# Forming all low weight parts on VectorE in a split-precision trunk layer, with the heads of one indexer visit turned

## The chip, the cores and the metric

The kernel runs on one core of a Trainium2 chip. The metric is device time in microseconds (us) of one execution. The engines named below are TensorE (PE, its weight loads PEld), VectorE (DVE), ScalarE (ACT), GpSimd (POOL) and SyncE (SP), which here only issues loads.

## The reference

One layer of a causal decoder trunk on x of 256 rows by 1024 columns, everything in 32-bit floats. Cut to what matters:

```python
proj = x @ w_in[i]                       # one projection, columns of all mixers
o_a = dsa_mixer(...)                     # 8 indexer heads -> top-k keys, 6 heads, one k and v
o_b = dilated_mixer(...)                 # 3 groups x 4 heads over shared k, v
o_c = moba_mixer(...)                    # 6 heads, causal (256 rows are a single block)
gates = sigmoid(x @ w_gate[i])           # 1024 x 3072
merged = gates_a*(o_a@w_br_a) + gates_b*(o_b@w_br_b) + gates_c*(o_c@w_br_c)
x = layer_norm(ALPHA*x + merged @ w_out)
h = square(relu(x @ w_up)) @ w_down      # 1024 -> 4096 -> 1024
ple = sigmoid(x @ w_ple_gate) * (p @ w_ple)
x = layer_norm(ALPHA*x + h + ple)
```

The indexer computes `index = sum over heads of iw * relu(iq . ik)` and keeps the best 64 keys of each row; attention of the first mixer is masked to these.

## The kernel before

**Products in two parts.** Each 32-bit product is made of three faster ones. A matrix w is split into a rounded high part (`whi`) and the rest (`wlo` = w − `whi`); x likewise into `xh` and `xl`. TensorE adds up hi·hi, hi·lo and lo·hi in PSUM (function `prod`, matmuls of L189, 128x256 each).

**Weight units.** Weights come from HBM as units of at most 512 KB (128x1024), each loaded by SyncE into one of five `raw` buffers. `Weights._split` (L95 to L126) then copies the unit on ScalarE to `whi` (L112, L110 later) and subtracts to get `wlo` (L119 where the part lies in one piece, L123 where it lies in pieces of 128 columns, class `Apart`, whose `runs` joins equally spaced pieces into one instruction). The subtraction is divided by columns: 0 to c on VectorE and c to n on GpSimd, with

```python
c = n if by == "v" else by * n // 1024
```

The first 58 units get `by` from `add` (L215): 640 (the constant `DV`, L41), and 615 for c units; all later ones get "v", VectorE alone. A unit is split four units before its use (`AHEAD`), and a part pool of five buffers holds them.

**The order of units.** The table `TASKS` (L44) lists them: 18 units of the q/k projections (numbers), 24 gate units (g, 1024 columns), 8 units of two branch matrices (c, 640 columns), 4 units each of value projections (va, 656 columns; vb, 768), then 4 of branch a (768) and 4 of the output matrix. A g or q/k unit is laid out as five pieces 160 columns apart and three pieces 128 apart; 640 is where that spacing changes. `fill` puts g and c units between the heads of attention.

**Around attention.** `feat` makes the queries and keys of a pair of heads; `logits` (L336) makes the scores of one or two pairs with 128x128 and 128x256 matmuls (L347). Its first matmul is free, and all that follow are held in program order among TensorE's instructions that are so pinned. The indexer loop (L508 to L518) calls it twice, each time for two pairs, and adds each head's part to `idx` (L515 on VectorE, L518 on GpSimd). Of each later head: bias and maximum on VectorE (L416), exponentials on ScalarE (L419), the reciprocal of the sum (L406, VectorE), scaling (L408, ScalarE), transposes on TensorE (L388), the split of the transposed probabilities (L389 ScalarE, L390 VectorE), the products with v (L392, L393), their sum from PSUM (L396 ScalarE, L397 and L398 VectorE), and for a pair its split (L401 ScalarE, L402 VectorE), which is the operand `op` of the c and a units. A g unit ends in a sigmoid step (L311 ScalarE) and, with branch products, a gated sum (L326, L327 on VectorE). After that come the output product, layer norm, the up and down matrices, and the last norm.

**What sets the order.** Each engine's instruction order is made by a scheduler that plays the program on modelled durations; priorities (`high_priority`), pins (`keep_in_program_order`) and `issue_after` bind it. A changed duration or engine in one step therefore also moves other instructions.

Of the kernel before, what the change touches and what calls it, by code (L numbers as in the profile page):

```python
# [37 lines left out]

AHEAD = 4
FIRST = 4  # L40
DV = 640  # L41


TASKS = ("4 va 5 g 6 7 g 8 g g 9 g 10 11 g 12 g g vb g 13 14 g g 15 16 g g 17 18 g g "  # L44
# [99 lines left out]
def hybrid_layer(ctx: ExitStack, tc: tile.TileContext, x0, xn, pT, wqk, wva, wvb, wg, wbc, wba,  # L144
# [33 lines left out]
    t = banks.tile([128, 512], F32, name="b4", tag="b4")  # L178
# [52 lines left out]
    for t in TASKS:  # L231
        if t == "va":
            u_va = [add(wva[i], 656) for i in range(4)]
        elif t == "vb":
            u_vb = [add(wvb[i], 768, at=(56, 56)) for i in range(4)]
        elif t in "gcao":
            u, w, n = {"g": (u_g, wg, 1024), "c": (u_bc, wbc, 640), "a": (u_ba, wba, 768),
                       "o": (u_out, wout, 1024)}[t]
            u.append([add(w[len(u)], n, at=(40, LOW[t]) if t in LOW else (0, 0),
                          by=615 if t == "c" else DV)])  # L240
        else:
            u_q.append([add(wqk[int(t) - FIRST], 1024, at=(40, LOW["g"]))])

# [89 lines left out]
            next(side, None)  # L333
        return ps

    def logits(k, *qs):  # L336


        ss = [next(ps_s if n < 3 else ps_t)[:, 0:384] for n in range(2 * len(qs))]
        with tc.high_priority(offset=500):  # L340
            for b in range(2):
                c = slice(b * 128, (b + 1) * 128)
                for n, q in enumerate(qs):
                    for i, (x, y) in enumerate(((1, 0), (0, 0), (0, 1))):
                        for h in (1, 0):
                            d = slice(64 * h, 64 * h + 64)
                            m = pe.matmul(ss[2 * n + h][:, QC[b]], lhsT=q[d, x, c],  # L347
                                          rhs=k[d, y, 0:128 * (b + 1)], start=i == 0, stop=i == 2)
                            if b or n or i or not h:
                                tc.keep_in_program_order(m)  # L350
        return ss

# [115 lines left out]
    with ExitStack() as begin:  # L468
# [25 lines left out]
        iq = [q_pair(ps, 0.125) for ps in first]  # L494
# [3 lines left out]
    kI, kA = k_pair(ps[0:64], ps[0:64]), k_pair(ps[64:128], ps[64:128])  # L498
# [7 lines left out]

    values(u_va, 328, 0, 5, True)
    for j in range(4):  # L508
        s = s[2:] if j % 2 else logits(kI, iq[j], iq[j + 1])
        r = wk2.tile([128, 768], F32, name="ri", tag="eb")  # L510
        r = r.rearrange("p (h k) -> p h k", h=2)
        for h in range(2):
            act.activation(r[:, h], s[h], AF.Relu)
            n = 2 * j + h
# [21 lines left out]
    for j in range(2):  # L536
        ps = feat(5 + 4 * j)
        k = k_pair(ps)
        fill("g")
        qs = []  # L540
# [16 lines left out]
    for j in range(3):  # L557
        ps = feat(13 + 2 * j)
        k = k_pair(ps)
# [566 lines left out]
```

## Time and profile before

| | |
|---|---|
| runs, us | 428.67, 430.38, 428.92 (median 428.92) |
| profiled execution, us | 428.66 (span 426.9) |
| granted TensorE clock | 0.998 |
| busy, share of span | PE 98%, PEld 89%, DVE 82%, ACT 65%, POOL 28% |
| HBM | 84.30 MB moved, 197 GB/s mean |

The span runs from the first to the last instruction; 1.76 us of the execution lie outside it. POOL's busy time stands mostly in one group, the 50 subtractions of L123 with 68.4 us. In the rows shown below the two leading numbers are start and duration in us, "x3" counts joined instructions, and what stands in brackets is the idle time just before and the instruction that ended it.

### The profile page before, as it was taken

How to read it: one execution, taken by the hardware profiler on the slowest of the kernel's cores; microseconds unless marked ns; L12 is line 12 of the kernel's file. 1: busy time of each engine (PE TensorE's matmuls, PEld its weight loads, DVE VectorE, ACT ScalarE, POOL GpSimd, SP SyncE). 2: the span in 40 equal slices, each digit the busy share in tenths (PEclk: the TensorE clock that was granted, in tenths of full speed). 3: DMA queues.
4: the chain of work that ended last, by engine and by line, in shares of the span. 5: the costliest groups of instructions: out<-in, count | busy, mean ns of one | idle time of the engine just before them, and what ended most of it. 6: DMA issues, size and time to landing. Idle time of an engine off the chain costs nothing.

```text
span 426.9 us, 7810 instructions
## 1 busy us (share of the span) xinstructions
PE 417.1 (98%) x2804; PEld 378.1 (89%) x2804; DVE 351.1 (82%) x645; ACT 279.6 (65%) x531; POOL 118.9 (28%) x127
## 2 busy tenths in 40 slices
PE   8999999999999999999999999999999999999993
PEld 8989999999999999999887888888888888788883
DVE  5968758898676689879967889989998798999755
ACT  6777385585888777858414668887888666567310
POOL 1668474173544556500010002242220000000001
PEclk9999999999999999999999999999999999999999
DMA  8895966567463327587851776785665376646402
GB/s 294 301 327 161 286 222 189 164 201 269 130 181 126 131 63 259 145 267 276 292 206 49 236 257 197 210 291 191 187 207 152 117 266 216 190 147 230 164 2 99
DMA packets 28157, 84.30 MB, mean 197 GB/s; under 512 B 2977, under 2 KB 6985, under 8 KB 27733
## 3 DMA queue, kind: packets, MB, share of 16 engines
q1 hardware_dynamic: 26880, 79.54, 57.0%
q10 hardware_dynamic: 1140, 4.19, 2.8%
q8 instruction: 22, 0.36, 0.4%
q14 instruction: 19, 0.15, 0.1%
q0 software_dynamic: 96, 0.06, 0.0%
HBM read 81.88 MB, written 1.90 MB: 196 GB/s over the span
## 4 chain that ended last, share of the span: by engine, by line
PE 78%; DVE 5%; DMA 4%; issue 2%; ACT 2%; SPq 0%; POOLq 0%; DVEq 0%; POOL 0%; ACTq 0%
PE mm L189 34%; PE b L189 19%; PE mm L891 14%; PE mm L893 7%; DMA xr<-in_wdn_dram 4%; PE b L347 2%; DVE wlo L119 2%; PE b L388 1%; PE b L392 1%; ACT whi L112 1%; DVE Y L853 1%; ACT ri L517 1%; PE b L393 0%; DVE wlo L123 0%; DVE st L701 0%
## 5 line engine op out<-in xcount | busy, mean ns | idle before, releaser
L112 ACT CAST whi<-raw 128x1024 fp32r<-128x1024 f32 (+3 forms) x92 | 89.9, 988 | 38.2 <-PE b L189 14.7
L123 DVE TENSOR_TENSOR wlo<-raw,whi 128x256 fp32r<-128x256 f32 (+3 forms) x118 | 96.4, 840 | 16.6 <-ACT whi L112 13.9
L189 PE MATMUL mm<-xh,whi 128*128 128x256 f32 x336 | 90.2, 280 | 0.0
L189 PE MATMUL mm<-xl,whi 128*128 128x256 f32 x336 | 88.1, 278 | 0.0
L123 POOL TENSOR_TENSOR wlo<-raw,whi 128x384 fp32r<-128x384 f32 (+1 forms) x50 | 68.4, 1377 | 70.2 <-ACT whi L112 65.5
L189 PE MATMUL mm<-xh,wlo 128*128 128x256 f32 x336 | 80.6, 281 | 0.2 <-DVE k L299 0.2
L189 PEld LDWEIGHTS mm<-xh,whi 128*128 128x128 f32 x336 | 63.1, 188 | 0.8
L891 PE MATMUL mm<-x,whi 128*128 128x512 f32 x256 | 63.4, 389 | 0.0
L189 PEld LDWEIGHTS mm<-xl,whi 128*128 128x128 f32 x336 | 63.1, 188 | 0.1
L189 PEld LDWEIGHTS mm<-xh,wlo 128*128 128x128 f32 x336 | 57.8, 188 | 0.8 <-DVE k L299 0.4
L189 PE MATMUL b<-whi,store 128*128 128x512 f32 x168 | 54.1, 389 | 0.0
L891 PEld LDWEIGHTS mm<-x,whi 128*128 128x128 f32 x256 | 45.7, 188 | 7.5
L119 DVE TENSOR_TENSOR wlo<-raw,whi 128x1024 fp32r<-128x1024 f32 (+2 forms) x38 | 43.2, 1159 | 3.7 <-ACT whi L112 3.6
L708 POOL TENSOR_TENSOR rs<-rs,half 128x1 f32<-128x1 f32 x4 | 3.4, 843 | 147.5 <-DVE rs L707 147.5
L110 ACT CAST whi<-raw 128x256 fp32r<-128x256 f32 x64 | 36.9, 617 | 10.0 <-PE mm L891 5.4
L189 PEld LDWEIGHTS b<-whi,store 128*128 128x128 f32 x168 | 31.5, 188 | 6.4
L893 PEld LDWEIGHTS mm<-x,wlo 128*128 128x128 f32 x256 | 33.8, 188 | 2.5
L893 PE MATMUL mm<-x,wlo 128*128 128x256 f32 x256 | 34.2, 276 | 0.0
L189 PE MATMUL b<-wlo,store 128*128 128x512 f32 x84 | 32.8, 391 | 0.3 <-DVE wlo L119 0.3
L914 POOL TENSOR_TENSOR a<-a 128x128 f32<-128x128 f32 x7 | 5.3, 757 | 61.5 <-ACT a L877 55.6
L189 PE MATMUL mm<-op,whi 128*128 128x256 f32 x128 | 22.4, 280 | 0.0
L189 PE MATMUL b<-whi,x 128*128 128x512 f32 x64 | 20.5, 395 | 0.0
(223 smaller groups left out, 824.2 us busy)
## 6 DMA issues: line engine op xcount, KB each, us to landing
raw<-in_wup_dram SPq DMA_DIRECT2D x32, 512.0 KB
raw<-in_wg_dram SPq DMA_DIRECT2D x24, 512.0 KB
raw<-in_wqk_dram SPq DMA_DIRECT2D x18, 512.0 KB
raw<-in_wdn_dram SPq DMA_DIRECT2D x18, 512.0 KB
raw<-in_wout_dram SPq DMA_DIRECT2D x8, 512.0 KB
raw<-in_wpg_dram SPq DMA_DIRECT2D x8, 512.0 KB
T<-tabd SPq DMA_DIRECT2D x24, 128.0 KB
xr<-in_wdn_dram SPq DMA_DIRECT2D x6, 512.0 KB
```

The costliest lines, as they stand in the source:

```text
L110: i = nc.scalar.copy(blocks(hi, a, b), blocks(r, a, b))
L112: i = nc.scalar.copy(hi, r)
L119: i = e.tensor_tensor(lo[:, x], r[:, x], hi[:, x].bitcast(F32), op=ALU.subtract)
L123: i = e.tensor_tensor(blocks(lo, *x), blocks(r, *x), blocks(hi, *x).bitcast(F32), op=ALU.subtract)
L189: i = pe.matmul(ps, lhsT=a[x], rhs=b[y], start=first and n == 0, stop=last and n == 2, skip_group_check=more)
L347: m = pe.matmul(ss[2 * n + h][:, QC[b]], lhsT=q[d, x, c], rhs=k[d, y, 0:128 * (b + 1)], start=i == 0, stop=i == 2)
L388: pe.transpose(t[:, 128 * i:128 * i + 128], P[:, 128 * i:128 * i + 128], ident)
L392: pe.matmul(v, lhsT=V[:, 0, vh], rhs=pt[:, :, 0:256], start=True, stop=False)
L517: act.mul(r[:, h, QC[0]], r[:, h, QC[0]], iw[:, 0, n:n + 1])
L891: pe.matmul(ps, lhsT=hi[:, c], rhs=x1[:, :, k], start=k == 0, stop=False)
L893: pe.matmul(ps[:, :, 0], lhsT=lo[:, c], rhs=x1[:, :, k, 0], start=False, stop=k == KT - 1)
L914: pool.tensor_tensor(sums[2], a11, a21, op=ALU.subtract)
```

## The change

Two things. `DV` becomes 1024 and c units use it too, so c = n for every unit and all low parts are formed by VectorE; GpSimd no longer subtracts. A unit in pieces then takes as many VectorE instructions as it has spacings: 640 + 384 columns for g and q/k units, 512 + 128 for c units. And `logits` takes the order of the two heads of a pair as an argument, (1, 0) as before by default; the second call of the indexer loop (j = 2) passes (0, 1).

```diff
-DV = 640
+DV = 1024
...
             u.append([add(w[len(u)], n, at=(40, LOW[t]) if t in LOW else (0, 0),
-                          by=615 if t == "c" else DV)])
+                          by=DV)])
...
-    def logits(k, *qs):
+    def logits(k, *qs, hs=(1, 0)):
...
-                        for h in (1, 0):
+                        for h in hs:
                             d = slice(64 * h, 64 * h + 64)
                             m = pe.matmul(ss[2 * n + h][:, QC[b]], lhsT=q[d, x, c],
                                           rhs=k[d, y, 0:128 * (b + 1)], start=i == 0, stop=i == 2)
-                            if b or n or i or not h:
+                            if b or n or i or h != hs[0]:
                                 tc.keep_in_program_order(m)
...
-        s = s[2:] if j % 2 else logits(kI, iq[j], iq[j + 1])
+        s = s[2:] if j % 2 else logits(kI, iq[j], iq[j + 1], hs=(1 - j // 2, j // 2))
```

The scheduler's order moves with it. TensorE keeps its first 182 matmuls in place and its last 1,176 instructions, from the merges of the branch products on; VectorE has 643 instructions in place of 584, GpSimd 65 in place of 90.

**TensorE, the second indexer visit.** Names: b0 to b3 are PSUM banks, k and q the indexer's key and two query pairs, mm the accumulator of a projection. Before, the 24 L347 follow one another; this is their beginning:

```order
L189 MATMUL mm_561<-xl_113,whi_389 128x256
L189 MATMUL mm_561<-xh_112,wlo_390 128x256
L347 MATMUL b1_516<-k_373,q_285 128x128
L347 MATMUL b0_515<-k_373,q_285 128x128
L347 MATMUL b1_516<-k_373,q_285 128x128
L347 MATMUL b0_515<-k_373,q_285 128x128
L347 MATMUL b1_516<-k_373,q_285 128x128
L347 MATMUL b0_515<-k_373,q_285 128x128
L347 MATMUL b3_518<-k_373,q_288 128x128
L347 MATMUL b2_517<-k_373,q_288 128x128
```

With the change, at the same place:

```order
L347 MATMUL b0_511<-k_369,q_285 128x128
L347 MATMUL b1_512<-k_369,q_285 128x128
L347 MATMUL b0_511<-k_369,q_285 128x128
L347 MATMUL b1_512<-k_369,q_285 128x128
L347 MATMUL b0_511<-k_369,q_285 128x128
L347 MATMUL b1_512<-k_369,q_285 128x128
L189 MATMUL mm_557<-xh_112,wlo_386 128x256
L189 MATMUL mm_557<-xl_113,whi_385 128x256
L189 MATMUL mm_557<-xh_112,whi_385 128x256
L347 MATMUL b2_513<-k_369,q_288 128x128
L347 MATMUL b3_514<-k_369,q_288 128x128
```

Bank 0 now comes ahead of bank 1, and three projection matmuls stand after the first six; the other 18 L347 follow in one piece.

**ScalarE, ahead of the first c unit.** e and den are a head's scores and sums, ov and b4 its product with v, pt1 its transposed probabilities. Before:

```order
L401 CAST op_129<-o_2001 128x256
L419 ACTIVATE e_2399,den_2401<-e_2399,mx_2400 128x128
L419 ACTIVATE e_2399,den_2401<-e_2399,mx_2400 128x256
L408 ACTIVATE e_2399<-e_2399,r_2406 128x128
L408 ACTIVATE e_2399<-e_2399,r_2406 128x256
L396 COPY ov_2195<-b4_2192 64x512
L389 CAST pt1_116<-b3_2272 128x384
```

With the change:

```order
L401 CAST op_129<-o_1993 128x256
L419 ACTIVATE e_2391,den_2393<-e_2391,mx_2392 128x128
L419 ACTIVATE e_2391,den_2393<-e_2391,mx_2392 128x256
L419 ACTIVATE e_2481,den_2483<-e_2481,mx_2482 128x128
L419 ACTIVATE e_2481,den_2483<-e_2481,mx_2482 128x256
L408 ACTIVATE e_2391<-e_2391,r_2398 128x128
L408 ACTIVATE e_2391<-e_2391,r_2398 128x256
L408 ACTIVATE e_2481<-e_2481,r_2488 128x128
L408 ACTIVATE e_2481<-e_2481,r_2488 128x256
L396 COPY ov_2187<-b4_2184 64x512
L389 CAST pt1_116<-b3_2264 128x384
```

Exponentials and scaling of a second head now stand ahead of L396; before, they came after it.

**VectorE, the last pair of heads before the merges.** op is the operand of the last branch product, mm a gated sum, wlo low parts of the last units. Before:

```order
L397 TENSOR_TENSOR ov_2733<-b4_2730,ov_2733 64x512
L398 TENSOR_TENSOR o_2623<-ov_2733 64x256
L123 TENSOR_TENSOR wlo_2867<-raw_2864,whi_2866 128x6x128
L402 TENSOR_TENSOR op_129<-o_2623,op_129 128x256
L123 TENSOR_TENSOR wlo_2898<-raw_2895,whi_2897 128x6x128
L326 SCALAR_TENSOR_TENSOR mm_2901<-G_114,mm_2901 128x256
```

With the change:

```order
L397 TENSOR_TENSOR ov_2725<-b4_2722,ov_2725 64x512
L326 SCALAR_TENSOR_TENSOR mm_2893<-G_114,mm_2893 128x256
L398 TENSOR_TENSOR o_2615<-ov_2725 64x256
L326 SCALAR_TENSOR_TENSOR G_114<-G_114,mm_2893 128x256
L326 SCALAR_TENSOR_TENSOR mm_2918<-G_114,mm_2918 128x256
L327 TENSOR_TENSOR G_114<-G_114,mm_2893 128x256
L123 TENSOR_TENSOR wlo_2915<-raw_2912,whi_2914 128x6x128
L402 TENSOR_TENSOR op_129<-o_2615,op_129 128x256
```

L402 now stands behind four gated steps and one subtraction where one subtraction stood between L398 and it.

## The prediction

> **What bounds the kernel now.** First the head of the page, its engine shares, and the list of TensorE's waits.
>
> ```profile
> span 426.9 us, 7810 instructions
> PE 417.1 (98%) x2804; PEld 378.1 (89%) x2804; DVE 351.1 (82%) x645; ACT 279.6 (65%) x531; POOL 118.9 (28%) x127
> ```
>
> ```profile
> PE b L180 <- POOL ident masks.py:199: 1.7, 1, 1.7
> PE b L189 <- DVE wlo L119: 0.3, 1, 0.3
> PE mm L189 <- DVE wlo L123: 0.3, 1, 0.3
> PE mm L189 <- DVE k L299: 0.2, 1, 0.2
> ```
>
> TensorE is busy for 98% of the span. Once the kernel has started, it waits three times, for 0.8 us together, and each time for VectorE. A shorter elementwise path can therefore give back very little; a longer one can only bring new waits. Two of these waits lie in the part that the change touches. What each costs is read from the starts of the matmuls around it (start, duration):
>
> ```profile
> 38.41 0.28 PE L189 MATMUL mm<-xh,wlo 128*128 128x256 f32 x1
> 38.93 0.38 PE L189 MATMUL mm<-xh,wlo 128*128 128x256 f32 x1 [0.25 <-DVE k L299]
> 39.16 0.28 PE L189 MATMUL mm<-xh,whi 128*128 128x256 f32 x1
> 39.27 0.28 PE L189 MATMUL mm<-xl,whi 128*128 128x256 f32 x1
> ...
> 155.97 0.51 PE L189 MATMUL mm<-op,whi 128*128 128x256 f32 x2
> 156.72 0.50 PE L189 MATMUL mm<-op,wlo 128*128 128x256 f32 x2 [0.25 <-DVE wlo L123]
> ```
>
> Undisturbed matmuls start 0.11 us apart (39.16 to 39.27). The first wait costs .52 − .11 = 0.41 us. At the second, two matmuls end their turn at 155.97 + .22 = 156.19, and the next starts at 156.72: 0.53 us.
>
> Which engine sets the pace of the low parts is seen where VectorE and GpSimd work on one weight unit (start, duration, engine):
>
> ```profile
> 42.97 1.02 POOL L123 TENSOR_TENSOR wlo<-raw,whi 128x384 fp32r<-128x384 f32 x1 [0.92 <-ACT whi L112]
> 45.74 1.64 POOL L123 TENSOR_TENSOR wlo<-raw,whi 128x384 fp32r<-128x384 f32 x1 [1.74 <-ACT whi L112]
> ```
>
> ```profile
> 42.98 1.69 DVE L123 TENSOR_TENSOR wlo<-raw,whi 128x640 fp32r<-128x640 f32 x1 [1.48 <-ACT whi L112]
> 45.69 0.83 DVE L123 TENSOR_TENSOR wlo<-raw,whi 128x640 fp32r<-128x640 f32 x1 [0.68 <-ACT whi L112]
> ```
>
> Whichever starts first has its lone time (1.02 for GpSimd, 0.83 for VectorE); the other takes about the sum (1.69, 1.64). In effect the two work one after the other, and a shared unit takes 1.65 to 1.7 us from copy to last column. The Trainium skill ("SBUF — State Buffer", section "Who interferes with whom") says why: GpSimd shares a port pair with VectorE under an exclusive lock. These four durations agree; by that rule GpSimd's share never saved time, which speaks for rival B below.
>
> **What the change costs VectorE.** The groups of its subtractions (count | busy, mean ns | idle before):
>
> ```profile
> L123 DVE TENSOR_TENSOR wlo<-raw,whi 128x640 fp32r<-128x640 f32 x42 | 44.1, 1052 | 13.1 <-ACT whi L112 12.7
> L119 DVE TENSOR_TENSOR wlo<-raw,whi 128x1024 fp32r<-128x1024 f32 x30 | 36.0, 1218 | 3.7 <-ACT whi L112 3.6
> ...
> L123 DVE TENSOR_TENSOR wlo<-raw,whi 128x256 fp32r<-128x256 f32 x32 | 14.2, 443 | 1.7 <-ACT whi L110 1.7
> ```
>
> 1218 − 443 over 768 columns is 1.01 ns a column. So 384 columns take .443 + 128 × .00101 = 0.57, 512 take 0.70, 128 take 0.31. A g or qk unit was one instruction of 640 columns, 1.05 on average because 0.22 of it is waiting for GpSimd; it becomes 640 + 384 = .83 + .57 = 1.40, so +0.35, 42 times: 14.7 us. A c unit goes from .57 to .70 + .31 = 1.01, +0.44, eight times: 3.5 us. The eight value units add at most .29 each (288 columns at 1.01 ns): 2.3. VectorE's 351 us become about 370. Before 150 us this has room: weights are split four units ahead. Nearest to full is this window (columns: PE, PEld, DVE, ACT, POOL busy):
>
> ```profile
> 150.00:180.00 30.00, 29.75 (x256) 29.01 (x256) 26.63 (x66) 23.42 (x54) 19.24 (x18) 1.00 0.47 155
> ```
>
> VectorE has 3.37 us free in those 30. About seven g and five c units are split there: 7 × .35 + 5 × .44 = 4.65 us more. Of the shown 26.63 part is waiting for the lock, already taken off in these prices. VectorE can do without the missing 1.28 us only by falling behind by that much or using work formed earlier. That is the core of rival C.
>
> Now the path of TensorE, place by place, from the start to 190 us; from the merges on its order is unchanged (the last 1,176 of its instructions).
>
> **Term 1, the wait at 38.93.** VectorE before it:
>
> ```profile
> 31.10 1.89 DVE L515 SCALAR_TENSOR_TENSOR idx<-ri,iw,idx 128x256 f32<-128x256 f32 x3
> 32.91 1.08 DVE L123 TENSOR_TENSOR wlo<-raw,whi 128x640 fp32r<-128x640 f32 x1
> 33.91 3.07 DVE L515 SCALAR_TENSOR_TENSOR idx<-ri,iw,idx 128x256 f32<-128x256 f32 x4
> 36.90 1.64 DVE L123 TENSOR_TENSOR wlo<-raw,whi 128x640 fp32r<-128x640 f32 x1
> ```
>
> Three L515 take 0.63 each, so four would take 2.52, not 3.07; 0.55 is lock. The two units lose .24 more lock each way: 1.08 + 1.64 = 2.72 against 2 × 1.40 = 2.80, +.08. Net k (L299) comes .55 − .08 = 0.47 earlier, and the wait of 0.41 goes. Bounds: −0.41 to 0 (if L515's extra has another cause). I take **−0.41**.
>
> **Term 2, the second indexer visit.** Before, its 24 L347 matmuls are one block:
>
> ```profile
> 46.39 1.64 PE L347 MATMUL b<-k,q 64*128 64x128 f32 x24
> 47.96 0.39 PE L189 MATMUL mm<-xh,whi 128*128 128x256 f32 x1
> 48.19 0.28 PE L189 MATMUL mm<-xl,whi 128*128 128x256 f32 x1
> ```
>
> Behind the block the first L189 takes .39, and the next starts .23 after it instead of .11: leaving costs 0.12. I price an entry the same. In the changed order three L189 stand inside the block, so it is left and entered once more: 2 × .12 = **+0.24**; bounds 0 (the modelled ends misplace that start, and nothing is lost) to 0.24. Turning the heads alone adds no instruction and no wait and is priced at nothing: 24 matmuls of the same sizes. That it does nothing of its own is thus part of the forecast.
>
> **Term 3, the first c unit (156.72).** Its low part is the last thing of a long chain on ScalarE and VectorE:
>
> ```profile
> 150.40 0.40 ACT L419 ACTIVATE e<-e,mx 128x128 f32<-128x128 f32 x1
> 150.71 0.19 ACT L419 ACTIVATION_READ_ACCUMULATOR e<-e,mx 128x1 f32 x1
> 150.80 0.50 ACT L419 ACTIVATE e<-e,mx 128x256 f32<-128x256 f32 x1
> 151.20 0.19 ACT L419 ACTIVATION_READ_ACCUMULATOR e<-e,mx 128x1 f32 x1
> 151.62 0.80 ACT L408 ACTIVATE e<-e,r 128x128 f32<-128x128 f32 x2 [0.23 <-DVE r L406]
> 152.45 0.58 ACT L396 COPY ov<-b 64x512 f32<-64x512 f32 x1
> ```
>
> ```profile
> 153.06 0.68 DVE L397 TENSOR_TENSOR ov<-b,ov 64x512 f32<-64x512 f32 x1 [1.48 <-ACT ov L396]
> ...
> 156.12 2.02 DVE L123 TENSOR_TENSOR wlo<-raw,whi 128x384 fp32r<-128x384 f32 x3
> ```
>
> In the new order the second head's L419 pair and L408 pair stand ahead of L396. By the starts, one L419 pair takes .90 (rows of one kind overlap by .09), one L408 pair some .70 (its .80 less the tail), and the .23 of waiting for r (L406) is now covered by the other head's work: .90 + .70 − .23 = 1.37, L396 at 153.82 instead of 152.45. From L396 VectorE's first step follows in .61; then eight operations stood ahead of the low part (153.06 to 156.12, 3.06), now seven (2.68); then 512 columns (0.70) must be done before TensorE starts, where 384 were: .61 + 2.68 + .70 = 3.99, ready at 157.81. TensorE wants it after the same number of matmuls, at 156.19, so it waits 1.62 in place of 0.53: **+1.1**. Bounds: −0.53 (the second head's work finds its data later, lets L396 go first in effect, and the wait goes with the lock) to +1.4 (nothing is covered).
>
> **Term 4, the last attention pair before the merges.** VectorE there:
>
> ```profile
> 185.18 0.96 DVE L123 TENSOR_TENSOR wlo<-raw,whi 128x768 fp32r<-128x768 f32 x1
> 186.06 0.42 DVE L402 TENSOR_TENSOR op<-o,op 128x256 fp32r<-128x256 f32 x1
> ```
>
> L402 makes the operand of the a units. Before, TensorE had 57 matmuls between the last L393 and the merges (57 × .113 = 6.4 us); in the new order 44, 4.97 us. And L402 now stands behind an L326 whose matmuls are the 33rd of these (3.73 us), an L327 and one more 768-column subtraction. With .42 for each 128x256 step: 3.73 + .42 + .42 + .96 + .42 = 5.95, less .08 of overlap at each of three borders, 5.7. The wait is 5.7 − 5.0 = **+0.7**; bounds 0 (the matmuls ahead are slower by other waits, so VectorE catches up) to 0.98 (no overlap).
>
> Everything else is priced at nothing. The cover is the four units that are split ahead: a g unit feeds 24 matmuls, 24 × .113 = 2.7 us, so a low part is due some 10 us after its split, and +0.35 a unit disappears in that. With the cover gone each g unit would cost up to its +0.35. GpSimd's remaining steps (masks, three DMA issues, index and table adds) queue behind no subtraction any more; they come earlier, and none of TensorE's waits above is for them. SyncE's loads are released when raw buffers come free, a few tenths earlier or later; none of the waits is for a DMA either.
>
> Sum: −.41 + .24 + 1.1 + .7 = +1.63 against the profiled execution's 428.66 (span 426.9 and 1.76 around it), so **430.3**. The median of the runs, 428.92, lies 0.26 above the profiled one.
>
> **Rivals.** *B, the late places don't come true.* VectorE no longer pays the lock, so it is ahead wherever it was behind; terms 3 and 4 fall to −.53 and 0: −.41 −.53 + .24 = −0.70, 428.0. For it: 1.69 where 0.83 would do, in many units. Against it: the new places of L419 and L408 stand in the order itself, and ScalarE, on which they run, shows no lock.
>
> *C, VectorE becomes the bound between 150 and 180 us: slower than before.* The place is the run of c units: one feeds 15 matmuls, 1.7 us, so four units ahead are hardly 7 us there, and the first has none. The price is what the 30 us lack: 3.37 free against 4.65 added gives at least 1.28, and as the free time is not all usable, up to 4.65; the middle, 3.0, with terms 1 and 2 (−.17) and half of term 4 (.35) gives +3.2, **431.8**. It decides when the share of VectorE in that window passes some 96%, where the waits for ScalarE that it has now no longer fit. For it: 26.63 of 30 already. Against it: units formed ahead lend time, and what other operations lose to the lock (L515's .55 above) comes back.
>
> *D, clearly faster.* With all three waits gone, and term 2 at 0: 428.66 − .41 − .53 − .3 = 427.4, no lower. Under 426.8 needs something that no row shows.
>
> **How the numbers follow.** Forecast 0.40, B 0.27, C 0.27, D 0.06. About 0.5% (2.1 us, so 426.8 to 431.1) is what a measurement here can tell from no change. The forecast's bounds add up to −.94 (427.7) and +2.7 (431.4), so a tenth of it lies above the half per cent: .04. C's bounds are 1.28 and 4.65 with +.18: 430.1 to 433.5, eight tenths of it above: .22. Slower .26; faster D's .06; same the rest, .68. The range is 427.6 to 432.3: from the lower bound of the forecast, which holds B, to a little past the middle of C; D and C's upper four tenths (.11) are left out.
>
> **What the changed profile would show.** Term 1: no PE wait for k L299, L515 four times 2.5. Term 2: two L347 blocks of 6 and 18. Term 3: L396 after 153.5, and the PE wait for wlo L123 at the first c unit near 1.7 long. Term 4: a PE wait for op L402 just before 190 us. For B: none of these waits, DVE 640+384 in 1.4 without a gap. For C: DVE over 29 of the 30 us and a row of PE waits for wlo L123. Wrong altogether would be a changed start of SyncE's loads, or a different duration of the 128x256 matmul.

## The result and the profile after

The changed kernel takes 432.81 us (median of 5), the kernel before beside it 429.77 us: 1.0077 times as long, 95% interval 1.0058 to 1.0097. A second comparison of the same two gave 1.0070 (1.0054 to 1.0086). So the change costs 3.0 to 3.3 us. That is slower by more than the 0.5% of the prediction, in the direction of the forecast, and beyond its range: 430.3 was forecast, 427.6 to 432.3 was the range.

The page of the changed kernel (span, engine shares) and the list of TensorE's waits:

```profile
span 430.1 us, 7695 instructions
PE 419.2 (97%) x2804; PEld 379.6 (88%) x2804; DVE 361.6 (84%) x695; ACT 279.5 (65%) x531; POOL 44.5 (10%) x69
```

```profile
PE b L180 <- POOL ident masks.py:199: 1.7, 1, 1.7
PE b L392 <- DVE pt L390: 1.0, 1, 1.0
PE mm L189 <- DVE wlo L123: 0.7, 1, 0.7
```

Two waits of 1.0 and 0.7 us, next to each other, stand where there was one of 0.3. By the page VectorE runs 695 instructions in place of 645 and GpSimd 69 in place of 127: the 50 more and 58 fewer that follow from the edit. (The counts given with the change, 643 for 584 and 65 for 90, do not agree with these.) VectorE's subtractions (groups with their shapes; count, busy us, mean ns of one):

```profile
L123 DVE TENSOR_TENSOR wlo<-raw,whi 128x640 fp32r<-128x640 f32 x42 | 35.1, 835 | 11.1 <-ACT whi L112 11.1
L123 DVE TENSOR_TENSOR wlo<-raw,whi 128x384 fp32r<-128x384 f32 x42 | 24.9, 594 | 0.0
...
L402 DVE TENSOR_TENSOR op<-o,op 128x256 fp32r<-128x256 f32 x8 | 3.8, 476 | 0.0
```

The two instructions of a g or q/k unit take .835 + .594 = 1.43 us by these means, where the prediction said 1.40. But the second starts before the first has ended, so an undisturbed pair takes 1.28 us. As a whole VectorE gained 10.5 us of busy time (351.1 to 361.6) and not the 20 that the prediction added up. The durations alone add up to 15.2 us more: L398, L515 and L402 together take 2.8 us less (L402 from 563 to 476 ns), and the value units take no more than before (7.1 us against 7.5). The other 4.7 us are this overlap of neighbouring instructions.

Where the time went is best read from a count of matmuls, as both programs have 2,804 of them in nearly the same order. Each column is the time from the start of one matmul to the start of a later one, in us, worked out from the traces:

```
matmul from        15     50    170    262    320    600   1000   1290   1340   1400   1600   1680   1900   2500
       to          50    170    262    320    600   1000   1290   1340   1400   1600   1680   1900   2500   2803
before           4.03  14.96   9.86   7.09  30.61  47.92  32.96   6.46   6.69  23.33   9.19  48.67 107.01  65.59
after            5.03  14.96  10.45   7.08  30.62  47.79  32.99   8.27   6.53  23.24   9.97  48.69 107.01  64.98
after, 2nd trace 5.40  14.96  10.45   7.08  30.62  47.79  32.99   8.27   6.53  23.24   9.99  48.69 107.01  64.98
before, 2nd tr.  5.09  14.96   9.88   7.13  32.00  48.39  32.95   6.46   6.67  23.33   9.19  48.67 107.01  64.98
```

Three stretches carry the change and repeat to 0.02 us: 170 to 262 (+0.59), 1290 to 1340 (+1.81) and 1600 to 1680 (+0.78). With the small ones between (170 to 1680) the sum is 2.8 us, against the first trace of before. The first and the last column differ as well, and so do the two of 320 to 1000 in one trace (by 1.9 us), but between two executions of the same program: they are chance. The profiled execution of before, on which the prediction was built, happened to have the shortest start of all.

**170 to 262, the indexer visits.** TensorE before and after (start, duration); before:

```profile
30.04 1.64 PE L347 MATMUL b<-k,q 64*128 64x128 f32 x24
```

after:

```profile
31.98 0.55 PE L347 MATMUL b<-k,q 64*128 64x128 f32 x6
32.46 0.39 PE L189 MATMUL mm<-xh,wlo 128*128 128x256 f32 x1
32.68 0.28 PE L189 MATMUL mm<-xl,whi 128*128 128x256 f32 x1
32.80 0.28 PE L189 MATMUL mm<-xh,whi 128*128 128x256 f32 x1
33.01 1.31 PE L347 MATMUL b<-k,q 64*128 64x128 f32 x18
```

The block is in two pieces, as the order said. Around it the changed program lost 0.40 us; another 0.18 went in the first visit, where an L461 pair now stands inside the projection matmuls.

**1290 to 1340.** ScalarE before:

```profile
148.15 0.48 ACT L389 CAST pt<-b 128x384 fp32r<-128x384 f32 x1 [0.57 <-PE b L388]
148.88 1.05 ACT L112 CAST whi<-raw 128x1024 fp32r<-128x1024 f32 x1 [0.25 <-PE mm L189]
```

and after, up to L396:

```profile
150.17 1.05 ACT L112 CAST whi<-raw 128x1024 fp32r<-128x1024 f32 x1 [0.40 <-PE mm L189]
151.24 0.48 ACT L389 CAST pt<-b 128x384 fp32r<-128x384 f32 x1
...
152.55 0.40 ACT L419 ACTIVATE e<-e,mx 128x128 f32<-128x128 f32 x1 [0.25 <-DVE mx L416]
...
154.33 1.48 ACT L408 ACTIVATE e<-e,r 128x128 f32<-128x128 f32 x4
155.83 0.58 ACT L396 COPY ov<-b 64x512 f32<-64x512 f32 x1
```

TensorE after, at the same place:

```profile
156.82 0.28 PE L189 MATMUL mm<-xh,wlo 128*128 128x256 f32 x1
158.05 0.50 PE L392 MATMUL b<-pt,V 128*128 128x512 f32 x1 [0.95 <-DVE pt L390]
...
158.83 0.50 PE L189 MATMUL mm<-op,whi 128*128 128x256 f32 x2
159.98 0.51 PE L189 MATMUL mm<-op,wlo 128*128 128x256 f32 x2 [0.65 <-DVE wlo L123]
```

L396 starts at 155.83 instead of 152.45. TensorE itself was 1.53 us later by then (its 1,300th matmul, 155.16 against 153.63), so L396 is 1.85 us late relative to it. Two rows of ScalarE make that: the four L419 and four L408, of which the prediction spoke, and the copy L112, which now stands ahead of L389 and not behind it. VectorE's L390, and behind it L416, wait for this L389. How the delay reaches TensorE is seen on VectorE (busy us of PE, PEld, DVE, ACT, POOL; before, then after):

```profile
153.00:157.00 4.00, 3.75 (x31) 3.46 (x31) 3.94 (x10) 3.63 (x7) 2.27 (x3) 1.00 0.00 0
```

```profile
153.00:157.00 4.00, 4.00 (x35) 3.85 (x33) 1.81 (x9) 3.95 (x14) 1.36 (x2) 1.00 0.00 0
157.00:165.00 8.00, 6.40 (x52) 5.99 (x51) 8.00 (x19) 4.88 (x8) 0.00 (x0) 1.00 0.38 119
```

VectorE stands idle for more than half of the four microseconds in which L396 is awaited, and is then busy without a gap until 165 us (before, 7.94 of these 8 us). So it is full just there in both kernels, and what it could not do ahead comes late. (The unit that is waited for is the third c unit; the prediction and the expectations call it the first.)

**1600 to 1680, ahead of the merges.** TensorE, and VectorE's L327 and L402:

```profile
193.30 0.99 PE L189 MATMUL mm<-op,whi 128*128 128x256 f32 x4
...
194.49 0.88 PE L189 MATMUL mm<-op,whi 128*128 128x256 f32 x3
```

```profile
193.32 0.41 DVE L327 TENSOR_TENSOR G<-G,mm 128x256 f32<-128x256 f32 x1
193.65 0.95 DVE L123 TENSOR_TENSOR wlo<-raw,whi 128x768 fp32r<-128x768 f32 x1
194.52 0.41 DVE L402 TENSOR_TENSOR op<-o,op 128x256 fp32r<-128x256 f32 x1
```

Four matmuls take .62 undisturbed and three .50, so .37 and .38 are waiting: 0.75 us. The first ends with VectorE's gated sum L327 (at 193.73; the next matmul starts at 193.78), the second with L402 (at 194.93; 194.98), which has the subtraction of 0.95 ahead of it.

### The profile page after: what moved, and what is told of

It is laid out like the page before. It is cut to its first block, busy times and chain, and to the rows that moved or that the text cites. A ratio compares the mean times of both kernels' runs of the same rounds, so it can differ in the third digit from the quotient of the medians.

```text
span 430.1 us, 7695 instructions
## 1 busy us (share of the span) xinstructions
PE 419.2 (97%) x2804; PEld 379.6 (88%) x2804; DVE 361.6 (84%) x695; ACT 279.5 (65%) x531; POOL 44.5 (10%) x69
## 4 chain that ended last, share of the span: by engine, by line
PE 85%; DVE 4%; DMA 3%; issue 2%; ACT 2%; SPq 1%; ACTq 0%; POOLq 0%; DVEq 0%; POOL 0%
PE mm L189 35%; PE b L189 25%; PE mm L891 13%; PE mm L893 7%; DMA raw<-in_wqk_dram 3%; PE b L347 2%; DVE wlo L123 1%; PE b L388 1%; ACT whi L112 1%; SPq L480 1%; PE b L392 1%; ACT ri L513 1%; DVE idx L515 0%; PE b L393 0%; DVE st L701 0%
## 5 line engine op out<-in xcount | busy, mean ns | idle before, releaser
L123 DVE TENSOR_TENSOR wlo<-raw,whi 128x640 fp32r<-128x640 f32 (+5 forms) x168 | 110.6, 700 | 16.0 <-ACT whi L112 13.6
L112 ACT CAST whi<-raw 128x1024 fp32r<-128x1024 f32 (+3 forms) x92 | 90.1, 990 | 38.1 <-PE b L189 13.5
L189 PE MATMUL mm<-op,whi 128*128 128x256 f32 x128 | 23.6, 283 | 0.2
L189 PEld LDWEIGHTS mm<-op,whi 128*128 128x128 f32 x128 | 19.0, 188 | 1.1 <-DVE op L402 0.3
L189 PEld LDWEIGHTS b<-wlo,store 128*128 128x128 f32 x84 | 15.8, 188 | 3.2
```

What stands on the lines that cost most here:

```text
L112: i = nc.scalar.copy(hi, r)
L123: i = e.tensor_tensor(blocks(lo, *x), blocks(r, *x), blocks(hi, *x).bitcast(F32), op=ALU.subtract)
L189: i = pe.matmul(ps, lhsT=a[x], rhs=b[y], start=first and n == 0, stop=last and n == 2, skip_group_check=more)
```

## The experiments

Two readings were to be told apart. "The order moved": the scheduler, seeing other durations, put instructions at a few places in another order, and TensorE waits there. "VectorE's load": VectorE has too much to do after 150 us, and the order only says where the wait shows. The times of all kernels stand beside the kernel before on the same chip, as ratio and 95% interval; "stretch A" is matmuls 1290 to 1340 (6.46 us before, 8.27 after), "late stretch" 1290 to 1680 (45.66 and 48.02).

### What belongs to chance, and the parts alone

The kernel before again, with no edit:

> The kernel before, unchanged, for its own spread and a second trace. Two differences between the two profiled executions lie where nothing was changed: in the one of after the first matmuls of L492 keep a spacing of 0.21 us until 7.2 us instead of until 5.0 (0.95 us lost), and the wait of TensorE for wlo L119 near 370 us (0.6 us) is missing. Theory 'chance of one execution': this second trace of the old kernel shows another length of the slow start and perhaps no wait at 370; its time is within 0.3% of the kernel before. Rival 'belongs to the change': the slow start ends at 5.0 us and the wait at 370 is 0.5 to 0.6 us as before.

1.0000 (0.9989 to 1.0012). Its start is slow until 7.0 us and its wait at 370 us is absent (64.98 in the last column): both differences are chance of one execution. TensorE's first matmuls of this execution (start, duration):

```profile
5.62 0.84 PE L492 MATMUL b<-xl,sh 128*128 128x256 f32 x3
6.26 0.94 PE L492 MATMUL b<-xh,sl 128*128 128x256 f32 x4
```

The changed kernel again:

> The changed kernel, unchanged, beside the three that follow. Theory 'chance of one execution': the slow start ends at another time than 7.2 us, and the loss against before without it is 2 to 2.8 us. Rival 'the slow start belongs to the change': it ends at 7.2 us again, and the loss is 3 to 3.4 us.

1.0070 (1.0054 to 1.0086), with every stretch from 170 to 1900 as in its first trace. The loss is 2.8 us by the stretches and 3.0 by the medians: above the upper end of the first theory's 2 to 2.8 or just at it, and the start differs again (5.40 against 5.03). The rival falls as far as the start goes; the 0.6 us of the last column belonged to before's one trace.

The turn alone: the argument `hs` and its call, with `DV = 640` and 615 kept.

```diff
-        s = s[2:] if j % 2 else logits(kI, iq[j], iq[j + 1])
+        s = s[2:] if j % 2 else logits(kI, iq[j], iq[j + 1], hs=(1 - j // 2, j // 2))
```

> The heads of the second indexer visit turned, the subtractions shared with GpSimd as before. The order then differs from before only in one of TensorE's projection matmuls, which stands ahead of the 24 logits instead of behind them. Theory 'the order moved' and the prediction: 0, within 0.3 us. Rival 'the turn costs time of its own': some 0.4 us, what the second visit lost in the changed kernel.

1.0001 (0.9990 to 1.0012), and each stretch within 0.04 of before. The turn alone does nothing.

The subtractions alone: `DV = 1024` and `by=DV`, the heads not turned.

> All low parts on VectorE, the heads not turned. It differs from the changed kernel only in the second indexer visit, whose 24 logits stand in four pieces (1, 5, 1, 17) in place of two (6, 18). Theory 'the order moved': the changed kernel's time plus 0.2 to 0.5 us, so 3 to 4 us slower than before; the turn mends a part of what the splits break. Rival 'the turn is part of the loss': the time is below the changed kernel's by some 0.4 us.

1.0066 (1.0053 to 1.0079), the same as the whole change. Its second visit is in four pieces and takes 0.86 us longer than in the changed kernel (11.31 against 10.45), and 0.51 of this comes back right behind it (6.57 against 7.08), where k is no longer waited for. What the turn gains is 0.35 us of one place; in the time it could not be told.

### GpSimd's lock

GpSimd writes zeros where it subtracted, in the kernel before, which leaves these low parts out of the products:

```diff
+                if e is nc.gpsimd:
+                    i = e.memset(blocks(lo, *x).bitcast(F32), 0.0)
+                    continue
```

> The kernel before, but GpSimd writes zeros into its columns of the low parts instead of subtracting (the low parts of these columns are thus left out of the products). VectorE keeps its 640 columns and GpSimd's operation reads nothing. Theory 'the lock costs the kernel before nothing': VectorE's 128x640 takes 0.83 to 0.9 us in place of 1.05, L515 0.63, and the time is that of the kernel before within 0.3%, at best the 0.4 at 39 us and the 0.4 at 157 us gone. Rival 'the lock costs': 1 us or more faster than before.

0.9983 (0.9973 to 0.9992): 0.7 us faster (0.3 to 1.2). VectorE's subtraction of 640 columns now takes its lone time (that kernel's lines are shifted by 6):

```profile
L129 DVE TENSOR_TENSOR wlo<-raw,whi 128x640 fp32r<-128x640 f32 x42 | 35.9, 855 | 23.8 <-ACT whi L112 20.4 <-PE b L399 2.0 <-POOL eb L455 0.6
```

855 ns against 1,052, though GpSimd still works on the same tiles. The Trainium skill ("SBUF — State Buffer", section "Who interferes with whom") says that GpSimd's reads contend with a VectorE instruction of two SBUF inputs, not its writes; these two numbers agree. On TensorE's path 0.52 us come back, all of it in 262 to 320 (6.57 against 7.09); 0.41 of it is the wait for k, which is gone. GpSimd's own part is shorter here too (0.42 us for a memset, 1.02 for a lone subtraction), so on this path the lock alone is worth at most this: little, and less than the orders that the change moved.

### The hold on GpSimd's queue

The table adds L584 and L585 on GpSimd stand in `issue_after(W.subs[-3])`: they are queued behind the third last subtraction, but only if that is on GpSimd. With the change it is on VectorE, and the hold is gone without a line of it being edited. GpSimd's rows before and after, the third and fourth add pair:

```profile
147.43 0.46 POOL L584 TENSOR_TENSOR ta<-T,am 128x128 f32<-128x128 f32 x1
...
155.71 0.47 POOL L584 TENSOR_TENSOR ta<-T,am 128x128 f32<-128x128 f32 x1
```

```profile
114.30 0.64 POOL L584 TENSOR_TENSOR ta<-T,am 128x128 f32<-128x128 f32 x1
...
144.73 0.46 POOL L584 TENSOR_TENSOR ta<-T,am 128x128 f32<-128x128 f32 x1 [29.10 <-DVE mx L416]
```

The fourth is the second head of the pair in question; its table is ready 11 us earlier, so its exponentials can stand ahead of L396. The kernel before without this hold:

```diff
-            with tc.issue_after(W.subs[-3]):
-                pool.tensor_tensor(ta[:, 0:128], T[:, n % 3, 128:256], am[:, 0:128], op=ALU.add)
...
+            pool.tensor_tensor(ta[:, 0:128], T[:, n % 3, 128:256], am[:, 0:128], op=ALU.add)
```

> The kernel before, with the hold taken away that queues GpSimd's table adds (L584, L585) behind its own subtraction; the subtractions stay shared. ScalarE's exponentials of the second head then stand ahead of L396, as in the changed kernel; VectorE's subtractions stay as they are. Theory 'the lost hold': the wait at the first c unit grows from 0.5 to 1.3 to 2 us, and the kernel is 0.8 to 1.5 us slower than before. Rival 'VectorE's longer subtractions make the wait': no more than 0.3 us slower.

1.0012 (0.9999 to 1.0025). Stretch A takes 6.99 (+0.53), and 0.19 is lost in 1400 to 1600. The lost hold costs about 0.6 us by the stretches, less than the theory's 0.8 and more than the rival's 0.3 (in the time it is not clear of zero): a cause, and not the main one.

The hold put back into the changed kernel, with a read of the low part:

```diff
+            z = pool.tensor_tensor(z, W.ends[-3].bitcast(F32), half, op=ALU.subtract)
-            with tc.issue_after(W.subs[-3]):
+            with tc.issue_after(z.ins):
```

> The changed kernel, with the hold put back: a one-column GpSimd operation reads the third last low part, and the table adds (L584, L585) stand behind it. L396 comes ahead of both heads' exponentials again; VectorE still makes all low parts. Theory 'the lost hold': the two waits near 158 and 160 us (1.1 and 0.8) shrink to 0.5 or less, 1.2 to 1.7 us faster than the changed kernel; the loss near 194 us stays, or grows by two matmuls (0.2). Rival 'VectorE is the bound there': the waits stay above 1.2 us in sum.

1.0080 (1.0060 to 1.0100), nothing won. Stretch A falls to 7.16, but 1340 to 1400 rises from 6.53 to 8.29: this hold is too late. The third add starts at 160.28, 13 us later than before the change, as the read ahead of it waits for VectorE. The theory's gain appears at its place and is lost again 5 us on, as the rival had it, but by the hold's own lateness; the run does not decide.

The same with a read of the high part, so that the hold ends with ScalarE's copy:

> The changed kernel with the hold put back in another way: the one-column GpSimd operation ahead of the table adds reads the third last unit's high part, so it waits for ScalarE's copy (as GpSimd's subtraction did before the change) and no longer for VectorE. ScalarE's order at the first c unit is then that of the kernel before. Theory 'the order moved': TensorE's matmuls 1290 to 1400 (the first c units; 13.15 us before, 14.80 in the changed kernel, 15.45 with the hold on the low part) take 13.2 to 13.7 us, and the kernel is 1.0 to 1.6 us faster than the changed one. Rival 'VectorE is the bound there': what is won at the first c unit is lost again within the next 30 us, as with the other hold; 14.5 us or more.

1.0067 (1.0048 to 1.0086). Matmuls 1290 to 1400 take 14.46, near the rival's 14.5 and far from the theory's 13.2 to 13.7. ScalarE's exponentials stand as before the change, and TensorE waits 1.5 us all the same (the copy L112 still stands ahead of L389). At this point VectorE's load looked the better reading.

### The place ahead of the merges

The last gate unit's matmuls behind the last L393, in the changed kernel:

```diff
-    fill("gggcc")
+    fill("gg")
+    with tc.issue_after(seen[0]):
+        fill("g")
+    fill("cc")
```

> The changed kernel, with the last gate unit's 24 matmuls queued behind the last L393 again (as before the change), so 54 matmuls stand between L393 and the branch a matmuls in place of 44, and L402 stands ahead of the gated steps. Theory 'the order moved': the loss of 0.8 us near 194 us goes; 0.6 to 0.9 us faster than the changed kernel, nothing else moves. Rival 'VectorE is late there by its load': the wait stays.

1.0073 (1.0052 to 1.0094). The wait in 1600 to 1680 is gone (9.19, as before), and 0.64 us come back in 1400 to 1600 (23.88), where TensorE, having nothing else to do, now waits for L390. No gain.

Both together, with the first and with the second kind of hold:

> The hold restored and the last gate unit behind L393, VectorE making all low parts. Theory 'the order moved': both gains add, 1.8 to 2.6 us faster than the changed kernel, within 0.2% of the kernel before, though VectorE is as loaded as in the changed kernel. Rival 'the load of VectorE': it stays 1.5 us or more behind the kernel before.

> The same, and the last gate unit's matmuls behind the last L393. Theory 'the order moved': matmuls 1290 to 1680 take at most 46.3 us (45.67 before, 48.01 in the changed kernel). Rival 'VectorE is the bound': 47.5 us or more; the waits move on to later places.

1.0095 (1.0079 to 1.0112) and 1.0064 (1.0045 to 1.0083). The late stretch takes 49.1 and 48.3 us. Five mends had left it at 47.9 to 49.1. That nothing is won is what the rival had said, though it did not always say where: the wait that it expected to stay ahead of the merges went, and others came.

### Which units

Only the c units wholly on VectorE, in the kernel before (`by=1024 if t == "c" else DV`):

> The kernel before, with only the eight c units' low parts wholly on VectorE, the other units shared. Theory 'the order moved, and VectorE's load in this stretch': the second indexer visit is as before; the first c unit needs 512 columns on VectorE before TensorE goes on, where it needed 384, so 0.1 to 0.3 us slower there; the table adds lose a part of their hold. 0 to 0.8 us slower than before. Rival 'c units are the loss': 1.5 us or more.

1.0026 (1.0011 to 1.0040). Stretch A +0.13, 1340 to 1400 +0.74 (a wait for L286), nothing else in the late stretch, and +0.41 behind it (1680 to 1900). In the time it is 1.1 us (0.5 to 1.7): a little above the theory's bounds, and below the rival's 1.5.

Units 0 to 39 wholly on VectorE, 40 to 57 shared as before; and the opposite half:

```diff
+        by = by if i < 40 else 615 if a[1] == 640 else 640
         return W.add(*a, by=by if i < 58 else "v", at=at)
```

> The changed kernel, but units 40 to 57 (used from about 150 us on: all c units and the late gate and q/k units) shared with GpSimd as before the change; units 0 to 39 stay wholly on VectorE. The orders at the first c unit and before the merges are those of the kernel before. Theory 'VectorE's load in the late stretch': matmuls 1290 to 1680 take 45.5 to 45.9 us (45.66 before, 48.02 in the changed kernel), although VectorE has all low parts until 150 us; what stays is the second indexer visit, 0.6. So 0.3 to 0.8 us slower than before. Rival 'load carried over from the early stretch': 46.5 us or more there.

> The opposite half: units 0 to 39 shared as before, units 40 to 57 wholly on VectorE. Theory 'VectorE's load in the late stretch': matmuls 1290 to 1680 take 47.5 to 48.5 us, the second indexer visit as before (9.9 us for matmuls 170 to 262), and the kernel is 2 to 2.8 us slower than before: the two halves add up to the whole change. Rival 'the order at the two places': ScalarE's order at the first c unit is here L419 four times, then L396 ahead of L408, as in the kernel without hold, which lost 0.5 us there; then 0.5 + 0.8, at most 1.3 us slower.

1.0021 (1.0008 to 1.0034) and 1.0049 (1.0029 to 1.0069). The early half keeps the late stretch at 45.53: VectorE's 40 earlier units cost nothing after 150 us. The late half has all of VectorE's extra work there, and takes 46.67: +1.0, of which 0.80 is the place ahead of the merges. That is the rival of its expectation ("0.5 + 0.8, at most 1.3"), the order, and not the 47.5 to 48.5 of the load. (The time alone, 2.1 us slower with 1.2 to 3.0, would have suited the load as well; it is the stretch that decides.) So the halves do not add up: 1.35 us of the late stretch need both, all in stretch A (6.84 with the late half, 8.27 with both). On ScalarE both together have two things there that neither half has: the copy L112 ahead of L389, and all four L408 ahead of L396.

The middle units alone, 14 to 39:

> The kernel before, with units 14 to 39 wholly on VectorE (used between about 45 and 150 us), those before and after shared. Every theory expects no loss, as neither the second indexer visit nor the stretch after 150 us is touched; the changed kernel was 0.13 us faster in matmuls 600 to 1000. From 0.3 us faster to no difference.

0.9985 (0.9970 to 1.0000). No loss anywhere, as expected; that it is faster than before is not shown.

### One copy

The copy of unit 46 is queued behind that L389, in the changed kernel; the rest of it is as it was.

```diff
+                if self.done == 46:
+                    ins = (*ins, self.pt[-2])
                 for x in ins:
                     held.enter_context(self.tc.issue_after(x))
```

> The changed kernel with one instruction moved: on ScalarE the copy L112 of unit 46 stands behind the last L389 ahead of it, as before the change, instead of before it (the scheduler then also puts L396 ahead of L408). Hold lost, VectorE's load and the place before the merges as in the changed kernel. Theory 'the order moved': matmuls 1290 to 1340 take 6.7 to 7.2 us in place of 8.27 (the kernel without hold 6.99, the late units alone 6.84), the kernel is 0.9 to 1.5 us faster than the changed one. Rival 'VectorE's load, grown by what the early units leave behind': 7.8 us or more.

1.0026 (1.0013 to 1.0039). Stretch A falls from 8.27 to 6.83, and nothing is lost behind it (6.53, 23.24 as in the changed kernel). ScalarE and TensorE there (the lines are shifted by 3, that of the copy by 1):

```profile
151.35 0.48 ACT L392 CAST pt<-b 128x384 fp32r<-128x384 f32 x1 [0.61 <-PE b L391]
151.72 1.05 ACT L113 CAST whi<-raw 128x1024 fp32r<-128x1024 f32 x1
...
155.13 0.58 ACT L399 COPY ov<-b 64x512 f32<-64x512 f32 x1
```

```profile
159.06 0.50 PE L192 MATMUL mm<-op,whi 128*128 128x256 f32 x2 [0.35 <-DVE G L330]
159.66 0.51 PE L192 MATMUL mm<-op,wlo 128*128 128x256 f32 x2
```

Where TensorE waited 1.1 and 0.8 us, it waits 0.5 and 0.3. In the time the kernel is 1.1 us slower than before (0.6 to 1.7), where the changed one was 3.0. The one constraint moved two things, since the scheduler then also put L396 ahead of the L408; which of the two is worth how much was not parted.

With the hold as well, and with all three mends:

> The same copy behind L389, and the hold by ScalarE's copy. Theory 'the order moved': matmuls 1290 to 1340 take 6.4 to 6.9 us (7.81 with the hold alone). Rival 'VectorE's load': 7.5 us or more.

> The copy behind L389, the hold by ScalarE's copy, and the last gate unit behind the last L393. VectorE still makes all low parts. Theory 'the order moved': matmuls 1290 to 1680 take 45.7 to 46.7 us (45.66 before, 48.02 in the changed kernel), and what is left against the kernel before is the second indexer visit: 0.5 to 1.5 us slower. Rival 'VectorE's load': 47.3 us or more, as with the two holds so far.

1.0021 (1.0004 to 1.0038) and 1.0009 (0.9997 to 1.0020). Stretch A is 6.45 and 6.49, as before the change. The late stretch is 46.10 and 46.05 against 45.66. With three places of the order mended, 1.97 of the 2.36 us are back, while VectorE still forms all low parts. VectorE has a larger share there than in the changed kernel, 44.1 of 46.05 us, 96%, against 42.8 of 48.02, 89% (before, 41.0 of 45.66, 90%). So over the stretch VectorE's load was not the bound at 89%; what the order had cost was the time in which VectorE had to stand idle. What is left, 0.4 us, may be load. Outside the late stretch these two traces lose more than the changed kernel's: the wait for k is 1.2 and 0.9 us, and 1680 to 1900 takes 49.59 and 49.09 us in place of 48.67. The latter is seen where the late gate units are shared as well (49.20 with the early half, 49.08 with the c units alone), and its cause stays open. The windows of the two kernels, 150 to 180 us (PE, PEld, DVE, ACT, POOL busy), the changed one first:

```profile
150.00:180.00 30.00, 28.40 (x247) 27.19 (x246) 26.74 (x73) 23.22 (x52) 1.42 (x2) 1.00 0.44 136
```

```profile
150.00:180.00 30.00, 29.55 (x256) 28.27 (x254) 28.46 (x74) 24.30 (x54) 4.48 (x9) 1.00 0.46 140
```

No kernel was clearly faster than the kernel before except the one that leaves low parts out.

## Why the prediction was right or wrong

The sum was +1.63 us. By the stretches, which are free of the chance at start and end, the change costs 2.8. Direction and mechanism were right, the size was too small, and the base was low. The steps that failed are in three terms. Term 3 counted one delay of L396, the second head's work, and left out the copy L112 that the new order puts ahead of L389: 1.81 us where 1.1 stood. Term 1 took VectorE's index work to start when it had started before: nothing came back where 0.41 was to. Term 2 priced one more piece of the logits at 0.24, and it cost 0.40, with 0.18 in the first visit besides. These and 0.08 of term 4 make 1.5 us; the small stretches gave 0.3 back.

- **What bounds the kernel**: right. In the late stretch the loss is TensorE waiting for VectorE, at two places. The second visit's 0.59 is no wait for another engine (none is listed there) but the price of changing between kinds of matmuls.
- **Term 1 (−0.41)**: wrong. The wait for k stays, 0.31 us where it was 0.41, and in other executions of kernels with all low parts on VectorE it was up to 1.2. What it said of L515 came true: the eight take 4.4 us in place of 5.2, and from the first L515 to k VectorE needs 7.93 us (32.00 to 39.93) in place of 8.86 (29.61 to 38.47), 0.93 less. The step that failed is that this work starts later. VectorE and ScalarE after:

```profile
26.69 1.28 DVE L123 TENSOR_TENSOR wlo<-raw,whi 128x640 fp32r<-128x640 f32 x2
...
32.00 0.71 DVE L515 SCALAR_TENSOR_TENSOR idx<-ri,iw,idx 128x256 f32<-128x256 f32 x1 [3.05 <-ACT iw L375]
...
33.42 1.54 DVE L123 TENSOR_TENSOR wlo<-raw,whi 128x640 fp32r<-128x640 f32 x2
34.89 3.64 DVE L515 SCALAR_TENSOR_TENSOR idx<-ri,iw,idx 128x256 f32<-128x256 f32 x6
38.45 1.56 DVE L123 TENSOR_TENSOR wlo<-raw,whi 128x640 fp32r<-128x640 f32 x2
```

```profile
29.61 0.87 ACT L513 ACTIVATE ri<-b 128x384 f32<-128x384 f32 x2 [1.46 <-PE b L347]
...
31.69 0.18 ACT L375 COPY iw<-mm 128x8 f32<-128x8 f32 x1
```

  VectorE waits 3.05 us for ScalarE's second copy of iw (31.69; before, 29.06). This copy stands behind the four L513 of the first visit, and they wait for its logits: the last 20 start at 27.92 instead of 25.72, as the L461 pair now stands ahead of them. So the first L515 is 2.39 us later, while TensorE is 1.57 later at the matmul ahead of the wait; this 0.82 uses up nearly all of the 0.93. The two pairs of 640 + 384 columns, at 1.54 and 1.56 us, are also above the 1.28 of an undisturbed pair, with GpSimd's index adds L518 running beside them. With GpSimd's subtractions replaced by writes, the wait is gone.
- **Term 2 (+0.24)**: right in kind, too small: 0.59. The row quoted for it, the 24 logits at 46.39 us, is a later block; the second visit stands at 30.04. An extra piece costs 0.40 and not 0.24: by the starts, the last projection matmul ahead of a piece takes 0.21 us, the last logits 0.20 and the first projection matmul behind it 0.22, where 0.11 is undisturbed, so time goes at more than two places. (With four pieces in place of two, the heads not turned, 0.86 more went.) The 0.18 of the first visit was missed: its rows were moved too, and that order was not read.
- **Term 3 (+1.1)**: right in place and chain, 0.7 too small in stretch A (+1.81). The second head's exponentials and scaling were priced about rightly, at 1.37: L396 is 1.85 late, and 0.62 of it is there already at the first L419 (152.55 against 150.40, with TensorE 1.53 later), which leaves 1.23. Missed was one row of the same list, L112 ahead of L389, which makes that 0.62. The copy and what followed from it, L396 ahead of L408 included, are worth 1.44. The lone lost hold costs 0.5. These two do not add up to their sum, as the places share one chain. (The wait of before was 0.42 and not 0.53, as its last matmul ahead starts at 156.19; the term is a difference and stays.)
- **Term 4 (+0.7)**: right: 0.78, at the place named, in two parts, the first of them for L327 ahead of L402. But mending that place alone gains nothing, which no term could have said.
- **VectorE's price per unit**: right as two durations (1.43 against 1.40), too high as busy time, since the two overlap (1.28). Its sum was too high for that reason above all: +10.5 us and not 20. What other operations got back, 2.8 us, was known to exist and left out.
- **Rival C**: at 431.8 it was nearest to the measured time, for a wrong reason. Its point of decision was a share above 96% in 150 to 180; the changed kernel has 26.74 of 30, no more than before (26.63), and the kernel with all mends has 28.46 with hardly a loss. VectorE is full in 157 to 165 us, where it nearly was before too, and busy for 9.90 of the next 10 (before, 8.42), in which TensorE does not wait.
- **The base**: the sum was set on the profiled execution, 428.66, which lay 0.26 below the median of three runs. With more runs the median of before is 429.1 to 429.8. Its start was the shortest of all twenty traces (4.03 us in the first column, 4.25 to 5.48 in the others). The 1.1 us to the 429.77 beside the result, and 1.2 of the terms, make nearly all of the 2.5 us between 430.3 and 432.8. (The forecast's upper bounds add up to 2.6, so 431.3, and not to 2.7.)

What is still open: how the 1.44 of stretch A divide between L112 and L396, whether the last 0.4 us is load, and where the 0.4 to 0.9 us in 1680 to 1900 of some kernels come from. That the second visit's loss is its order is read from the trace; no run puts that order back with all low parts on VectorE.

## What to carry to other kernels

When work is moved from one engine to another, look for constraints that were tied to the instruction that moved: a hold "behind that subtraction" applied to GpSimd's queue, and it vanished with no line of it touched. Where a scheduler decides the order, its moved rows on each engine of the chain have to be read one by one; one constraint that moved a 1 us copy behind a short operation of the chain, and let L396 go ahead, gave back 1.4 us of 2.8. A mended place that returns nothing does not prove that an engine is full: the next place of the same kind may be waiting behind it, and the test is to mend them all and see how busy that engine gets.

## What was not expected of the hardware

The first projection matmuls (L492, 128x256) start 0.21 us apart and later 0.11, and the step comes at another time in each execution of the same program: near 5.2 us in the first trace of before, at 7.0 in the second, 7.2 and 7.6 in the two of after. The granted clock of the profile shows 1.00 throughout. This alone moves one execution by about 1 us. The first trace of before, to set beside the rows of the second above (three matmuls take 0.34 us from 5.41 to 5.75 here, and 0.64 from 5.62 to 6.26 there):

```profile
5.41 0.51 PE L492 MATMUL b<-xl,sh 128*128 128x256 f32 x3
5.75 0.62 PE L492 MATMUL b<-xh,sl 128*128 128x256 f32 x4
```

The Trainium skill ("TensorE: Matmul & The Clock Gate", section "Part 1: The HAM clock gate") describes a free-running window of 3.4 us after which the clock doubles, so that the same kernel has a different number of slow matmuls each time; both spacings and the shift agree with it; the granted clock does not show it.
